# The first two rows of each partition stored from the scalar queue while the opening loads run: a top-2 expert dispatch

## The chip, the cores and the metric

The kernel runs on one core of one Trainium2 chip. The metric is the device time of one execution in microseconds (us); lower is better. A profile of one execution goes with it. Its span, from the first to the last instruction, is a little shorter than the device time, because the device time also holds the start and the end of the program.

Engines are named as the profile names them: DVE is VectorE, ACT is ScalarE, POOL is GpSimd, and SP is SyncE, which here only issues transfers. Each of the issuing engines has a queue of its own for DMA transfers; SPq stands for SP's issuing.

## The reference

For each of 16 x 1024 = 16,384 tokens, eight router logits give probabilities; the two largest are normalised to sum to one, and the token's row of 512 floats is written twice, scaled once by each of the two weights (the smaller first).

```python
def reference(x, router_logits, k):              # x: 16 x 1024 x 512, k = 2
    logits_max = np.max(router_logits, axis=-1, keepdims=True)
    probs = np.exp(router_logits - logits_max)
    probs = probs / np.sum(probs, axis=-1, keepdims=True)
    topk_indices = np.argsort(probs, axis=-1)[..., -k:]
    topk_probs = np.take_along_axis(probs, topk_indices, axis=-1)
    topk_probs = topk_probs / np.sum(topk_probs, axis=-1, keepdims=True)
    x_expanded = x[:, :, np.newaxis, :].repeat(k, axis=2)
    return (x_expanded * topk_probs[..., np.newaxis]).astype(np.float32)
```

Two of eight, normalised, need only the difference of the two largest logits and a sigmoid. What is left is movement: 33.6 MB of x are read, and 67.1 MB of output are written.

## The kernel before

Each of the 128 partitions holds 128 consecutive tokens ("rows"). A row of x is 2 KB, and a row of the output, with its two copies, is 4 KB. The rows are worked on in two groups of 64. A group's four loads of 16 rows fill the buffer `xs` (64 rows). Six multiplies make the output: 16 rows into the separate buffer `osp`, 16 rows into the lower half of `xs` itself (whose input has been used up by then), 8 and 8 rows into `osp` again, and 8 and 8 rows into the upper half of `xs`. Each is stored as soon as it is made. All transfers, loads and stores, are issued from the sync queue, in the order of the program.

```python
    GROUP = 64
    L = 16
    # ... x_v, o_v: partition p holds rows p*128 .. p*128+127
    logits = wpool.tile([P, M, E], F32)
    nc.sync.dma_start(logits, rl_v)
    WA = top2_weights(nc, wpool, logits, M, E)    # max/min tree on DVE, two sigmoids on ACT

    xs = wpool.tile([P, GROUP, D], F32)           # 64 rows, 128 KB in each partition
    osp = wpool.tile([P, L, 2, D], F32)           # 16 rows of output, 64 KB in each partition

    low = xs[:, : 2 * L, :].rearrange("p (r k) d -> p r k d", k=2)
    high = xs[:, 2 * L :, :].rearrange("p (r k) d -> p r k d", k=2)
    h = L // 2
    plan = [                                      # first row, rows, where the output is made
        (0, L, osp),
        (L, L, low),
        (2 * L, h, osp[:, :h]),
        (2 * L + h, h, osp[:, h:]),
        (3 * L, h, high[:, :h]),
        (3 * L + h, h, high[:, h:]),
    ]

    for g in range(M // GROUP):                   # two groups
        m0 = g * GROUP
        for r in range(0, GROUP, L):              # four loads of 16 rows
            nc.sync.dma_start(xs[:, r : r + L, :], x_v[:, m0 + r : m0 + r + L, :])
        for r, n, og in plan:
            rows = slice(m0 + r, m0 + r + n)
            nc.vector.tensor_tensor(
                og,
                xs[:, r : r + n, :].unsqueeze(2).to_broadcast([P, n, 2, D]),
                WA[:, rows, :].unsqueeze(3).to_broadcast([P, n, 2, D]),
                op=ALU.mult,
            )
            nc.sync.dma_start(o_v[:, rows], og)
```

The loads of the second group overwrite `xs`, so each of them waits for the stores that read that part of `xs`. The third multiply of a group overwrites the first half of `osp`, so it waits for the store of what the first multiply made.

Of the kernel before, what the change touches and what calls it, by code (L numbers as in the profile page):

```python
# [1 line left out]

# [4 lines left out]

F32 = mybir.dt.float32
ALU = mybir.AluOpType
ACTF = mybir.ActivationFunctionType  # L10
P = 128


def top2_weights(nc, pool, logits, M, E):

    hi, lo, n = None, None, E
    while n > 1:  # L20
        n //= 2
        if hi is None:
            a, b = logits[:, :, 0:n], logits[:, :, n : 2 * n]
            nhi = pool.tile([P, M, n], F32, tag=f"hi{n}")
            nlo = pool.tile([P, M, n], F32, tag=f"lo{n}")
            nc.vector.tensor_tensor(nhi, a, b, op=ALU.max)  # L26
            nc.vector.tensor_tensor(nlo, a, b, op=ALU.min)  # L27
        else:
            a, b = hi[:, :, 0:n], hi[:, :, n : 2 * n]
            nhi = pool.tile([P, M, n], F32, tag=f"hi{n}")  # L30
            nlo = pool.tile([P, M, n], F32, tag=f"lo{n}")
            tmp = pool.tile([P, M, n], F32, tag=f"tmp{n}")
            nc.vector.tensor_tensor(tmp, lo[:, :, 0:n], lo[:, :, n : 2 * n], op=ALU.max)  # L33
            nc.vector.tensor_tensor(nlo, a, b, op=ALU.min)  # L34
            nc.vector.tensor_tensor(nlo, nlo, tmp, op=ALU.max)  # L35
            nc.vector.tensor_tensor(nhi, a, b, op=ALU.max)  # L36
        hi, lo = nhi, nlo
    dlt = pool.tile([P, M], F32, tag="dlt")
    nc.vector.tensor_tensor(dlt, hi[:, :, 0], lo[:, :, 0], op=ALU.subtract)  # L39
    WA = pool.tile([P, M, 2], F32, tag="WA")  # L40
    nc.scalar.activation(WA[:, :, 0], dlt, ACTF.Sigmoid, scale=-1.0)  # L41
    nc.scalar.activation(WA[:, :, 1], dlt, ACTF.Sigmoid, scale=1.0)  # L42
    return WA


@with_exitstack
def kernel(
    ctx: ExitStack,
    tc: tile.TileContext,
    x: bass.AP,  # L50
    router_logits: bass.AP,
    k: bass.AP,
    out: bass.AP,
):
    nc = tc.nc
    B, S, D = x.shape
    E = router_logits.shape[-1]
    N = B * S
    assert int(k) == 2 and E == 8 and N % P == 0
    M = N // P  # L60

    GROUP = 64
    L = 16
    x_v = x.rearrange("b s d -> (b s) d").rearrange("(p m) d -> p m d", p=P)
    o_v = out.rearrange("b s k d -> (b s) k d").rearrange("(p m) k d -> p m k d", p=P)
    rl_v = router_logits.rearrange("b s e -> (b s) e").rearrange(
        "(p m) e -> p m e", p=P
    )

    wpool = ctx.enter_context(tc.tile_pool(name="wpool", bufs=1))  # L70
    logits = wpool.tile([P, M, E], F32)
    nc.sync.dma_start(logits, rl_v)  # L72
    WA = top2_weights(nc, wpool, logits, M, E)

    xs = wpool.tile([P, GROUP, D], F32)
    osp = wpool.tile([P, L, 2, D], F32)


    low = xs[:, : 2 * L, :].rearrange("p (r k) d -> p r k d", k=2)
    high = xs[:, 2 * L :, :].rearrange("p (r k) d -> p r k d", k=2)  # L80
    h = L // 2
    plan = [
        (0, L, osp),
        (L, L, low),
        (2 * L, h, osp[:, :h]),
        (2 * L + h, h, osp[:, h:]),
        (3 * L, h, high[:, :h]),
        (3 * L + h, h, high[:, h:]),
    ]

    for g in range(M // GROUP):
        m0 = g * GROUP
        for r in range(0, GROUP, L):
# [6 lines that stand above are left out]
                WA[:, rows, :].unsqueeze(3).to_broadcast([P, n, 2, D]),  # L100
                op=ALU.mult,
            )
            nc.sync.dma_start(o_v[:, rows], og)  # L103


# [1 line left out]
_INS = ['x', 'router_logits', 'k']  # L107
_OUTS = [((16, 1024, 2, 512), 'float32')]

_NUMBERS = {'k': 2}  # L110


# [26 lines left out]
```

## Time and profile before

| | |
|---|---|
| device time, median of 3 runs | 242.84 us (242.69 to 243.03) |
| device time of the profiled execution | 242.31 us |
| its span | 240.5 us |
| DVE busy | 142.0 us, 23 instructions |
| ACT busy | 1.8 us, 3 instructions |
| packets | 3,024, with 101.19 MB |
| multiply of 16 rows (16,384 elements in each partition) | 17.2 us |
| multiply of 8 rows (8,192 elements) | 8.7 us |
| load of 16 rows, 4,096 KB, issue to landing | 36.3 us, median of 8 |

In a profile, a line such as "DVE L97 TENSOR_TENSOR osp<-xs,WA" is an instruction of VectorE from line 97 that writes `osp` from `xs` and `WA`. The time from the issue of a transfer to its landing holds its wait behind the transfers ahead of it, so it is longer than the moving of its bytes alone. A row of digits gives the busy share, in tenths, of 40 equal slices of the span. The page's rate of data (GB/s) in a short slice can swing, as a packet's bytes are all counted where the packet starts.

### The profile page before, as it was taken

Reading aid. Unit: us, or ns where it says so; the run is one execution under the profiler, and the core shown is the slowest. Engines: PE = TensorE matmul, PEld = TensorE weight load, DVE = VectorE, ACT = ScalarE, POOL = GpSimd, SP = SyncE. Lnnn points to the kernel's source line nnn. Section 1 sums busy time; section 2 is a strip of 40 time slices with the busy share of each in tenths; the row PEclk is TensorE's granted clock in tenths of the full one; section 3 lists DMA queues with packets and bytes.
Section 4 is the critical chain, followed back from the end, with each engine's and each line's share of the span. In section 5 each row is a group of like instructions: output and inputs, shape, how many; then the busy total and the mean of one; then the engine's idle time right before and its main releaser. Section 6 shows DMA issues by size and latency. Waiting matters only on the chain.

```text
span 240.5 us, 112 instructions
## 1 busy us (share of the span) xinstructions
DVE 142.0 (59%) x23; ACT 1.8 (1%) x3; POOL 0.2 (0%) x4
## 2 busy tenths in 40 slices
DVE  3279999900399999400000899998007999990000
ACT  2000000000000000000000000000000000000000
POOL 0000000000000000000000000000000000000000
DMA  8999999898989899999999999999989898999995
GB/s 327 430 409 425 430 431 425 349 523 349 523 349 523 349 436 436 436 436 431 436 338 431 436 431 430 431 474 414 458 381 490 371 501 360 431 436 436 436 436 256
DMA packets 3024, 101.19 MB, mean 421 GB/s; under 512 B 336, under 2 KB 336, under 8 KB 464
## 3 DMA queue, kind: packets, MB, share of 16 engines
q1 hardware_dynamic: 3024, 101.19, 98.7%
HBM read 34.08 MB, written 67.11 MB: 421 GB/s over the span
## 4 chain that ended last, share of the span: by engine, by line
DMA 46%; DVE 36%; issue 7%; SPq 0%; DVEq 0%
DMA out_dram<-osp 27%; DVE osp L97 22%; DMA xs<-in_x_dram 19%; DVE xs L97 14%; SPq L72 0%; SPq L103 0%; DVEq L97 0%
## 5 line engine op out<-in xcount | busy, mean ns | idle before, releaser
L97 DVE TENSOR_TENSOR osp<-xs,WA 128x8192 f32<-128x8192 f32 (+1 forms) x6 | 69.0, 11534 | 70.1 <-DMA xs<-in_x_dram 40.3
L97 DVE TENSOR_TENSOR xs<-xs,WA 128x8192 f32<-128x8192 f32 (+1 forms) x6 | 69.2, 11536 | 0.2
L26 DVE TENSOR_TENSOR nhi<-logits 128x512 f32<-128x512 f32 x1 | 0.7, 693 | 4.0 <-DMA logits<-in_router_logits_dram 4.0
L41 ACT ACT_TABLE_LOAD x1 | 1.3, 1283 | 0.7 <-PEq L120 0.7
L36 DVE TENSOR_TENSOR nhi<-nhi 128x256 f32<-128x256 f32 (+1 forms) x2 | 0.7, 354 | 0.0
L34 DVE TENSOR_TENSOR nlo<-nhi 128x256 f32<-128x256 f32 (+1 forms) x2 | 0.7, 354 | 0.0
L33 DVE TENSOR_TENSOR tmp<-nlo 128x256 f32<-128x256 f32 (+1 forms) x2 | 0.7, 353 | 0.0
L35 DVE TENSOR_TENSOR nlo<-nlo,tmp 128x256 f32<-128x256 f32 (+1 forms) x2 | 0.7, 352 | 0.0
L27 DVE TENSOR_TENSOR nlo<-logits 128x512 f32<-128x512 f32 x1 | 0.7, 685 | 0.0
L41 ACT ACTIVATE WA<-dlt 128x128 f32<-128x128 f32 x1 | 0.3, 315 | 5.8 <-DVE dlt L39 5.8
L39 DVE TENSOR_TENSOR dlt<-nhi,nlo 128x128 f32<-128x128 f32 x1 | 0.3, 291 | 0.0
L42 ACT ACTIVATE WA<-dlt 128x128 f32<-128x128 f32 x1 | 0.3, 298 | 0.0
L120 POOL MEMSET const-bfloat16-1.0<- 128x1 bf16 x1 | 0.1, 101 | 0.0
L120 POOL MEMSET const-uint8-127<- 128x1 uint8 x1 | 0.1, 101 | 0.0
L120 POOL MEMSET const-float32-0.0<- 128x1 f32 x1 | 0.1, 98 | 0.2 <-issue 0.2
L120 POOL MEMSET const-float32-1.0<- 128x1 f32 x1 | 0.1, 98 | 0.0
## 6 DMA issues: line engine op xcount, KB each, us to landing
xs<-in_x_dram SPq DMA_DIRECT2D x8, 4096.0 KB, 36.3
out_dram<-osp SPq DMA_DIRECT2D x4, 4096.0 KB, 20.7
out_dram<-xs SPq DMA_DIRECT2D x4, 4096.0 KB, 22.7
logits<-in_router_logits_dram SPq DMA_DIRECT2D x1, 512.0 KB, 3.3
out_dram<-osp SPq DMA_DIRECT2D x2, 32.0
out_dram<-xs SPq DMA_DIRECT2D x2, 34.1
```

The source lines that it names most:

```text
L26: nc.vector.tensor_tensor(nhi, a, b, op=ALU.max)
L27: nc.vector.tensor_tensor(nlo, a, b, op=ALU.min)
L33: nc.vector.tensor_tensor(tmp, lo[:, :, 0:n], lo[:, :, n : 2 * n], op=ALU.max)
L34: nc.vector.tensor_tensor(nlo, a, b, op=ALU.min)
L35: nc.vector.tensor_tensor(nlo, nlo, tmp, op=ALU.max)
L36: nc.vector.tensor_tensor(nhi, a, b, op=ALU.max)
L39: nc.vector.tensor_tensor(dlt, hi[:, :, 0], lo[:, :, 0], op=ALU.subtract)
L41: nc.scalar.activation(WA[:, :, 0], dlt, ACTF.Sigmoid, scale=-1.0)
L42: nc.scalar.activation(WA[:, :, 1], dlt, ACTF.Sigmoid, scale=1.0)
L97: nc.vector.tensor_tensor(og, xs[:, r : r + n, :].unsqueeze(2).to_broadcast([P, n, 2, D]), WA[:, rows, :].unsqueeze(3).to_broadcast([P, n, ...
L120: nc = _bacc.Bacc("TRN2", target_bir_lowering=False, num_devices=1)
```

## The change

The first multiply of each group is cut in two: 2 rows, then the other 14. Each part gets a store of its own. In the first group the 2-row store is issued from the scalar queue instead of the sync queue. Its purpose is to let the first output leave for HBM while the opening loads are still running, without standing behind those loads in the sync queue. In the second group the 2-row store goes through the sync queue like the others (its first row is 64, not 0). Nothing else changes, and the computation stays whole.

```diff
     h = L // 2
+    e = 2
     plan = [
-        (0, L, osp),
+        (0, e, osp[:, :e]),
+        (e, L - e, osp[:, e:]),
         (L, L, low),
         (2 * L, h, osp[:, :h]),
         (2 * L + h, h, osp[:, h:]),
@@ in the loop over the plan @@
                 WA[:, rows, :].unsqueeze(3).to_broadcast([P, n, 2, D]),
                 op=ALU.mult,
             )
-            nc.sync.dma_start(o_v[:, rows], og)
+
+            queue = nc.scalar if rows.start == 0 else nc.sync
+            queue.dma_start(o_v[:, rows], og)
```

## The prediction

> **What bounds the kernel now.** I read the page's first three parts first, to see which engine is ever full.
>
> ```profile
> span 240.5 us, 112 instructions
> DVE 142.0 (59%) x23; ACT 1.8 (1%) x3; POOL 0.2 (0%) x4
> ...
> DMA  8999999898989899999999999999989898999995
> ...
> q1 hardware_dynamic: 3024, 101.19, 98.7%
> HBM read 34.08 MB, written 67.11 MB: 421 GB/s over the span
> ```
>
> VectorE (DVE) works 59% of the span. The 16 DMA engines are at 98.7%, on one queue (q1). The first digit of the DMA row is the start-up, the last the drain; nothing between shows a hole. Bytes are fixed by the problem, so the suspicion is that the kernel takes as long as 101.19 MB take.
>
> The chain of work that ended last seems to disagree (DVE 36%), so the waits come next: does a late VectorE ever leave the DMA engines without work? First the waits, then the timeline from 13 to 64 us (start, duration, engine, instruction):
>
> ```profile
> DVE osp L97 <- DMA xs<-in_x_dram: 40.3, 2, 34.3
> DVE osp L97 <- DMA out_dram<-osp: 29.8, 2, 15.7
> ...
> 13.79 17.23 DVE L97 TENSOR_TENSOR osp<-xs,WA 128x16384 f32<-128x16384 f32 x1 [5.98 <-DMA xs<-in_x_dram]
> 31.05 0.35 SPq L103 DMA_DIRECT2D out_dram<-osp  x1
> 31.05 17.22 DVE L97 TENSOR_TENSOR xs<-xs,WA 128x16384 f32<-128x16384 f32 x1
> 48.30 0.34 SPq L103 DMA_DIRECT2D out_dram<-xs  x1
> 63.95 8.69 DVE L97 TENSOR_TENSOR osp<-xs,WA 128x8192 f32<-128x8192 f32 x1 [15.67 <-DMA out_dram<-osp]
> ```
>
> VectorE waits for DMA, 40.3 + 29.8 us, never the reverse for long. The first store is issued at 31.05, but the four opening loads, issued by 3.0 us, are still draining: by the trace's packet records the last of them ends at 44.2 us, and the store's first packet starts at 43.4, right behind the loads on its engine. So the store was queued 12 us ahead of its turn. I checked the same for every later transfer (issue to landing is 20.2 to 42.9 us, while 4 MB need only 9.7): each is issued with at least one other still ahead of it. Counted from the packet records, the 16 engines together are idle 0.65 us on average between the first packet (1.75 us) and the last (239.2 us), nearly all of it in the uneven finish.
>
> Hence the sum: 2,048 packets of 32 KB at 1.213 us and 512 of 64 KB at 2.418 us, over 16 engines, are 155.3 + 77.4 = 232.6 us; the logits' 128 packets of 4 KB at 0.159 us add 1.3. That is 233.9 of the 237.4 us between first and last packet. The other 3.4 us are packets longer than usual: 0.4 us in the start-up, 1.48 us at 40 to 44 us (loads give way to stores), 1.31 us at 118 to 127 us (stores to loads), 0.15 us at 158 to 162 us (loads to stores again). The windows show the middle one (columns: stretch, us, busy time of DVE, ACT and POOL, clock, DMA share, GB/s):
>
> ```profile
> 44.20:63.50 19.30, 4.08 (x1) 0.00 (x0) 0.00 (x0) 1.00 1.00 435
> ...
> 117.50:128.00 10.50, 0.00 (x0) 0.00 (x0) 0.00 (x0) 1.00 1.01 381
> 128.00:156.20 28.20, 23.14 (x2) 0.00 (x0) 0.00 (x0) 1.00 0.99 429
> ```
>
> Stores alone move 435 GB/s, loads alone 429, and the stretch in which stores and loads of different engines meet 381.
>
> **What the Trainium skill says.** "DMA: Bandwidth & Descriptors", section "Issuing engines are not separate DMA queues": transfers started by the scalar, sync or gpsimd engine end on the same 16 DMA engines and interleave; a second issuer saves only sequencer time. The trace has little to save: SP's issues take 0.33 to 0.53 us each and overlap transfers. The same page, "Where 436 GB/s comes from", puts the fabric's ceiling at 435 GB/s; the 435 of the window above agrees, so the store stages have nothing left. The same page, "Queues, rings and completion order": an engine takes turns between its queue rows, a whole packet at a time. This kernel has one queue, so no run here shows it yet; my placing of the early store rests on it. "Perfetto Trace Analysis", section "DMA Optimizations", says that splitting may let the whole finish sooner if DMA engines are generally idle; here they are not.
>
> **The change part by part.**
>
> (1) VectorE, the split of 16 rows into 2 and 14, in both groups. 16,384 elements take 17.225 us and 8,192 take 8.690, so 1.0419 ns each plus 0.155 us. 2,048 elements: 2.29 us; 14,336: 15.09; together 17.38 instead of 17.23. The +0.15 us per group lies ahead of waits of 15.7 and 14.1 us for a store: hidden.
>
> (2) The early store, first group. VectorE ends the two rows at 13.79 + 2.29 = 16.1 us. ScalarE has been free since 8.4 us. SP's first issue at 0.73 had its first packet at 1.75, so packets start near 17.1. The store is 128 packets of 8 KB (2 rows x 2 copies x 2 KB), 8 for each engine. From the line through 4 KB (159 ns) and 32 KB (1,213 ns) one is 0.31 us. Alternating with load packets, 8 turns are 8 x (1.213 + 0.31) = 12.2 us: it lands near 29.5 us.
>
> (3) What that displaces. The loads lose 8 x 0.31 = 2.5 us: the second lands before 25 instead of 23.4, the third near 35.5 instead of 33.1, the fourth near 47 instead of 44.5. VectorE needs the second at 31.2 and the third at 64. The 14-row store, issued at 31.2, starts when the fourth load ends, 2.5 us later, and is shorter by 8 packets' 8 KB, 2.4 us. It lands where the whole store landed, 63.9 us, and from there on everything repeats. The early bytes are not extra transfer capacity; they have pushed others back.
>
> (4) Packet overhead. 64 KB at 2.418 becomes 8 KB at 0.310 plus 56 KB at 2.418 - 0.301 = 2.117: +9 ns, 8 times per engine, 0.07 us; with another completion record of 9 ns, 0.08 per group, 0.16 us in all. This lies on the bound.
>
> (5) The second group's 2-row store stays on the sync queue, behind loads; it gets only the overhead of (4).
>
> (6) The build's instruction order adds one condition to the third multiply: it waits for the early store as well as the 14-row store. By (2), 34 us before it matters. The rotation of DMA semaphores shifts by one per new transfer; every wait I followed is on a transfer that landed well earlier or was waited for anyway.
>
> Without mixing the sum is +0.16 us, 243.0.
>
> **Rivals.** *Reads and writes disturb each other.* In the stretch at 381 GB/s, against the 429 of the clean loads after it, 10.5 x (1 - 381/429) = 1.2 us are lost. The change makes some 12 us of interleaving from 17 to 29 us. At that rate it costs 12.2 x 0.112 = 1.4 us: 244.4. Worse: at 40 to 44 us each engine's last two load packets took about 2.0 us instead of 1.2. If all eight load packets between the early store's packets stretched by 0.75 us, that would be 6 us: 249. Against it: at 158 to 162 us some engines still loaded while others stored, for only 0.15 us. I put a few tenths into the central figure.
>
> *An easier turn from loads to stores.* If the 1.48 us at 40 to 44 us are the price of the first writes, starting them softly might save it: 241.5. Against it, the second turn cost a tenth of that with the same instructions, so the price is not fixed; and the turn is still there behind the early store.
>
> *The DMA engines read and write at once, so the early store rides free.* Then 8 x 0.31 = 2.5 us would be gained: 240.5. Against it: wherever engines work undisturbed, packets follow end to end, one at a time on each engine.
>
> *VectorE or a wait gets onto the path.* It would need over 10 us of delay to empty the queue; nothing here makes that.
>
> **Range and chances.** 243.0 plus some 0.2 us as the weighted share of mixing (loss likelier than gain) is 243.2. The times before span 0.34 us. The low end, 242.1, takes half of the cheaper turn; the high end, 245.2, the 1.4 us of mixing plus some. Faster by over 2% means below 238.0, hardly above the packets' floor of 233.9 plus both ends' 3.1 us: 0.02. Slower by over 2% means above 247.7, which only the harsh form of mixing reaches: 0.06. The rest, 0.92, is within.
>
> **What would show it.** A second DMA queue with 1.05 MB, its store issued near 16.1 and landing near 29.5 us (in step 2); were it near 19, it had priority, near 46, it stood behind the loads. Load packets stay at 1.213 us from 17 to 29 us (no mixing cost), or stretch. The third multiply starts at 63.9 +- 1.5 us, and DMA waits remain over 65 us. The stretch of 40 to 44 us, now near 46, says whether the turn got cheaper. I am wrong if the DMA row shows a hole, if load packets stretch over the whole interleaving, or if the span falls by over 2 us.

## The result and the profile after

The changed kernel takes 241.87 us (median of 4 runs, 241.72 to 241.93) where the kernel before took 242.94 us (median of 4, one run more than in the table of before; 242.69 to 243.37). The ratio is 0.9953, with a 95% interval of 0.9936 to 0.9970. The gain is small, and the interval is clear of 1. The forecast of 243.2 us had the wrong sign, and its low end of 242.1 us lies 0.23 us above the result. Measured again later, with 21 runs beside 43 of the kernel before, the ratio was 0.9983 (0.9976 to 0.9991), a gain of 0.4 us. These two intervals don't meet. The changed kernel's median hardly moved between the two comparisons (241.87 and 241.71 us), while the kernel before, at 242.94 us here, had medians of 242.16 to 242.35 us in all four later comparisons. So the 0.4 us are the better figure, and the first 1.07 us hold 0.6 to 0.8 us that belong to the first runs of the kernel before.

The page of the changed kernel, its first three parts:

```profile
span 240.2 us, 116 instructions
DVE 142.1 (59%) x25; ACT 1.8 (1%) x3; POOL 0.2 (0%) x4
...
DMA  7999999988989899999999999999999898999996
...
q1 hardware_dynamic: 3168, 100.14, 97.8%
q10 hardware_dynamic: 144, 1.05, 1.0%
HBM read 34.08 MB, written 67.11 MB: 421 GB/s over the span
```

The second queue (q10) is there with its 1.05 MB. The DMA row still has no hole, and the mean rate is the same 421 GB/s. Now the timeline of the changed kernel from 13 to 70 us, then the times from issue to landing of its first stores (in us, last column), then its longest waits:

```profile
13.92 17.29 DVE L99 TENSOR_TENSOR osp<-xs,WA 128x2048 f32<-128x2048 f32 x2 [6.05 <-DMA xs<-in_x_dram]
16.25 0.37 ACTq L107 DMA_DIRECT2D out_dram<-osp  x1
31.24 0.35 SPq L107 DMA_DIRECT2D out_dram<-osp  x1
...
63.21 8.69 DVE L99 TENSOR_TENSOR osp<-xs,WA 128x8192 f32<-128x8192 f32 x1 [14.74 <-DMA out_dram<-osp]
```

```profile
out_dram<-osp SPq DMA_DIRECT2D x2, 7168.0 KB, 31.8
out_dram<-osp ACTq DMA_DIRECT2D x1, 1024.0 KB, 16.6
```

```profile
DVE osp L99 <- DMA xs<-in_x_dram: 40.3, 2, 34.2
DVE osp L99 <- DMA out_dram<-osp: 29.3, 2, 14.7
```

The early store is issued at 16.25 us, as worked out, and lands at 16.25 + 16.6 = 32.9 us. The third multiply starts at 63.21 instead of 63.95 us. So 0.74 us have been won by then, where the forecast had nothing won. Other profiles agree: it starts at 63.95 to 64.05 us in three profiles of the kernel before, and at 63.17 us in a second one of the changed kernel. VectorE waits for DMA about as long as before, 69.6 us (70.1 before), which cost nothing then and cost nothing now.

**Where the time went.** One measure is used from here on. The packet records of a trace give each packet's duration, and a given size nearly always takes the same one: 4 KB 0.159 us, 8 KB 0.309, 16 KB 0.611, 32 KB 1.213, 56 KB 2.116, 64 KB 2.418. Whatever a packet takes beyond that, summed and divided by the 16 engines, is called *stretch*. It says how much later the engines are, on average, for packets that went slowly. As long as the engines have work throughout and end level, a stretch moves the end by as much. In the thirteen profiles of the table below this can be tried: the stretch after 14 us, taken from the mean end of the 16 engines, leaves 235.8 to 236.2 us each time.

The table gives the stretch in us by place; four more profiles are told in the text. The start-up before 14 us, with 0.26 to 0.62 us in each, is left out. "Early" is 14 to 32 us, where a small first store of the first group meets the loads; "turn 1" is 32 to 60 us, where the first group's loads end and its stores follow; "back" is where the second group's loads follow the first group's stores (75 to 133 us); "early 2" (133 to 150 us) and "turn 2" (150 to 170 us) are the same as "early" and "turn 1" in the second group. The last column is when the last of the 16 engines ended.

| kernel | early | turn 1 | back | early 2 | turn 2 | last end |
|---|---|---|---|---|---|---|
| before | 0.00 | 1.48 | 1.31 | 0.00 | 0.15 | 239.2 |
| before, again (two) | 0.01, 0.01 | 1.33, 1.37 | 0.66, 0.89 | 0.01, 0.00 | 0.48, 0.44 | 239.2, 239.2 |
| changed | 0.74 | 0.04 | 1.22 | 0.00 | 0.64 | 238.9 |
| changed, again | 0.64 | 0.00 | 1.20 | 0.00 | 0.18 | 238.5 |
| split, all on sync | 0.00 | 0.94 | 0.78 | 0.00 | 0.47 | 239.0 |
| first group only | 0.56 | 0.03 | 1.02 | 0.00 | 0.61 | 238.6 |
| both groups early | 0.57 | 0.00 | 0.77 | 0.37 | 0.01 | 238.2 |
| both groups early, again | 0.67 | 0.00 | 0.93 | 0.10 | 0.00 | 238.3 |
| both, 1 row | 0.16 | 0.66 | 0.97 | 0.00 | 0.24 | 238.5 |
| both, 4 rows | 1.07 | 0.00 | 0.87 | 0.72 | 0.00 | 239.8 |
| 8 rows, first group early | 1.03 | 0.89 | 0.73 | 0.00 | 0.33 | 240.0 |
| both early, one queue | 1.43 | 0.21 | 0.76 | 0.71 | 0.00 | 239.8 |

In the first group the kernel before pays 1.33 to 1.48 us in its three profiles, and the changed kernel 0.64 and 0.78. That is where the gain lies. The split's packet overhead takes 0.13 us back (the sum of all the usual durations is 234.10 us before and 234.23 after). The second group is as it was, apart from the wander of "back" and "turn 2", which differ by 0.3 to 0.65 us between profiles of one kernel. That is as much as the whole gain, so one profile alone would not show it; turn 1 wanders far less.

### The profile page after: what moved, and what is told of

Same layout as the page of the kernel before. It is cut to its first block, busy times and chain, and to the rows that moved or that the text cites. A ratio compares the mean times of both kernels' runs of the same rounds, so it can differ in the third digit from the quotient of the medians.

```text
span 240.2 us, 116 instructions
## 1 busy us (share of the span) xinstructions
DVE 142.1 (59%) x25; ACT 1.8 (1%) x3; POOL 0.2 (0%) x4
## 3 DMA queue, kind: packets, MB, share of 16 engines
q10 hardware_dynamic: 144, 1.05, 1.0%
## 4 chain that ended last, share of the span: by engine, by line
DMA 49%; DVE 32%; issue 7%; SPq 1%; DVEq 0%
DMA out_dram<-osp 26%; DMA xs<-in_x_dram 23%; DVE osp L99 18%; DVE xs L99 14%; SPq L96 0%; SPq L72 0%; SPq L107 0%; DVEq L99 0%
## 5 line engine op out<-in xcount | busy, mean ns | idle before, releaser
L99 DVE TENSOR_TENSOR osp<-xs,WA 128x8192 f32<-128x8192 f32 (+2 forms) x8 | 69.2, 8688 | 69.6 <-DMA xs<-in_x_dram 40.3
## 6 DMA issues: line engine op xcount, KB each, us to landing
out_dram<-osp ACTq DMA_DIRECT2D x1, 1024.0 KB, 16.6
```

What stands on the lines that cost most here:

```text
L99: nc.vector.tensor_tensor(og, xs[:, r : r + n, :].unsqueeze(2).to_broadcast([P, n, 2, D]), WA[:, rows, :].unsqueeze(3).to_broadcast([P, n, ...
```

## Experiments

Each changes the kernel before or the changed kernel by the lines shown, and the computation stays whole in all of them.

**Is it the split, the early store, or chance?** First, the split alone:

```diff
-            queue = nc.scalar if rows.start == 0 else nc.sync
+            queue = nc.sync
```

> Both splits into 2 and 14 rows kept, but every store from the sync queue, so that nothing is stored while the opening loads run. Theory (meeting the loads early is what helps: the first turn from loads to stores cost 1.48 us of stretched packets before, and 0.74 + 0.04 after): no gain left, ratio 1.000 to 1.001, and the stretch of about 1.5 us stands again at 40 to 44 us. Rival (the split helps: 8 KB packets at the head of the stores soften the turn): ratio 0.994 to 0.997 as with the whole change, and under 0.5 us of stretch at 40 to 44 us.

Measured: 242.19 us, ratio 1.0001 (0.9990 to 1.0012), and 0.94 us at turn 1. In time the split alone gives nothing, so the rival is out. The theory was not all right either: it had 1.5 us at turn 1. The 8 KB packets at the head of the stores may soften the turn (the third multiply starts at 63.67 us), and the overhead of 0.13 us takes part of that back; one profile can't settle it.

Next, the first group alone, with the second left unsplit:

```diff
-        for r, n, og in plan:
+        steps = plan if g == 0 else [(0, L, osp)] + plan[2:]
+        for r, n, og in steps:
```

> Only the first group is split, with its 2-row store from the scalar queue; the second group is as in the kernel before. Theory (early store alone): the whole gain, ratio 0.994 to 0.996, by 0.1 us better than the whole change because the second group's split overhead of 0.08 us is gone. Rival (the split): about half of the gain, 0.997 to 0.998.

And the whole change once more:

> The whole change again, beside the others on one chip. Both theories: ratio 0.994 to 0.997. A third theory, that the gain is the wander of the turns from run to run, expects a ratio that is not clear of 1.0, or packets stretched at other places than in the first profile (0.74 us at 18 to 24, 0.04 at 44, 1.21 at 118 to 126, 0.64 at 156 to 162 us).

Measured: 241.79 us, ratio 0.9984 (0.9975 to 0.9993), and 241.71 us, 0.9983 (0.9976 to 0.9991). Both numbers that I wrote down were too large, as they leaned on the first measurement. By the sizes they name, early_only even looks like the rival's half; but the comparison that counts is with the whole change measured beside it, and there the two are equal. So the whole gain is the early store of the first group. It is also clear of 1.0, and the stretch in the first group, 0.64 and 0.00 us, lies where it lay in the first profile, so it is no chance.

Then the second group's 2-row store from the scalar queue as well, measured twice:

```diff
-            queue = nc.scalar if rows.start == 0 else nc.sync
+            queue = nc.scalar if r == 0 else nc.sync
```

> The second group's 2-row store also goes from the scalar queue, so it too meets its group's loads (issued near 134 us, loads until 162 us). Theory (early meeting makes a turn cheap): a second gain where the second turn is dear; with 0.15 to 0.64 us at that turn, at most 0.6 us less, but the early meeting costs up to 0.7 us of its own: ratio 0.992 to 0.997. If only the very first write of the kernel is dear, nothing more is gained: the ratio of the whole change plus 0 to 0.003. The rival (the split) expects the same as the whole change.

> Both groups' 2-row stores from the scalar queue, again, beside its variants. If the early meeting is worth something at each turn: ratio 0.9955 to 0.998, better than the whole change by about 0.001, and no stretch of over 0.15 us near 44 and 160 us. If the first result was the wander of the runs: 0.9976 to 0.9991, as the whole change had on that chip.

Measured: 241.23 us, 0.9967 (0.9955 to 0.9979), and 241.30 us, 0.9966 (0.9954 to 0.9978). The same treatment pays again at the second turn, which falls to 0.01 and 0.00 us, for 0.37 and 0.10 us at the new early meeting: 0.38 and 0.10 us in all, where the turn alone cost 0.15 to 0.64 us in the versions without it. So it is not only the very first write that is dear. This version beats both kernels: beside its 241.23 us, the changed kernel took 241.71 us in the same comparison. Its page, second profile, and its early stores:

```profile
span 239.5 us, 116 instructions
...
q1 hardware_dynamic: 3024, 99.09, 96.7%
q10 hardware_dynamic: 288, 2.10, 2.1%
HBM read 34.08 MB, written 67.11 MB: 423 GB/s over the span
...
out_dram<-osp ACTq DMA_DIRECT2D x2, 1024.0 KB, 16.6
```

**Is the dear turn the rule?** The kernel before, twice more, for its turns:

> The kernel before once more, for its turns alone. If the first turn from loads to stores is dear as a rule: 0.9 to 1.5 us near 40 to 44 us. If 1.48 us was chance: under 0.8 us. The turn near 159 us, 0.15 us before, shows how far a turn wanders.

> The same again: 0.9 to 1.5 us near 40 to 44 us, or under 0.8 us if the first was chance.

1.33 and 1.37 us at the first turn: it is the rule. The second turn, 0.48 and 0.44 us, shows that the 0.15 of the first profile, on which the forecast leaned, was at the low end of what this turn costs: where the second group's first store is not early, it lies anywhere from 0.15 to 0.64 us in the table.

**Does more of it help?** I thought that a second queue's alternation would make every turn cheap, whatever the size. First the unsplit 16-row store from the scalar queue:

```diff
-            nc.sync.dma_start(o_v[:, rows], og)
+            queue = nc.scalar if rows.start == 0 else nc.sync
+            queue.dma_start(o_v[:, rows], og)
```

> No split; the first group's whole 16-row store (64 KB packets) goes from the scalar queue. It is issued near 31 us, while some 9 of the 128 load packets of each engine... counted from 31 to 44 us, are still to come, so it alternates with them. Theory (a turn is cheap where the two directions alternate from two queues, whatever the size): ratio 0.997 to 0.999, and no stretch of over 0.3 us where the loads end. Rival (it needs small packets, or a start long before the loads end): ratio 0.9995 to 1.001, with 0.9 to 1.5 us of stretched packets in all between 30 and 60 us.

(Each engine has 32 load packets in a group, not 128.) Measured: 243.50 us, ratio 1.0050 (1.0033 to 1.0068). The theory falls in this form. Stretch is 1.34 us at turn 1, at 32 to 37 us, where the store meets the loads: as dear as before. After that, 32 KB loads and 64 KB stores alternate at their usual durations. And one engine ends at 241.0 us, 1.9 us after the next.

The other extreme, all stores from the scalar queue (`queue = nc.scalar`):

> No split; all twelve stores from the scalar queue, all loads from the sync queue, so that stores and loads alternate at every change of direction, also where the second group's loads follow the first group's stores (1.0 to 1.3 us of stretch near 119 to 126 us so far). Theory: all three turns get cheap, total stretch 1.2 to 2.2 us instead of 2.6 to 3.4, ratio 0.993 to 0.998. Rival (each change costs much the same wherever it lies): stretch of 2.5 us or more in other places, ratio 0.999 to 1.003.

Measured: 245.06 us, ratio 1.0100 (1.0077 to 1.0123). Neither theory had this ratio. The total stretch, 3.55 us, is the rival's "2.5 us or more", but not the whole loss. The windows near the end show the rest (stretch, us, busy DVE, ACT, POOL, clock, DMA share, GB/s):

```profile
231.00:237.00 6.00, 0.00 (x0) 0.00 (x0) 0.00 (x0) 1.00 1.01 437
237.00:243.40 6.40, 0.00 (x0) 0.00 (x0) 0.00 (x0) 1.00 0.29 123
```

In the last 6.4 us the engines are busy for 29% only: nine have ended by 237.8 us, the others between 239.9 and 243.3. After a long alternation the engines are no longer level, and the slowest sets the end. In the kernel before all 16 end within 1.1 us. This profile and the one before it are of the slowest executions of their kernels (246.43 and 244.20 us), so the usual unevenness may be smaller. Why single engines fall behind I did not trace.

A second queue that meets no loads at first, the store from the lower half of the buffer (`queue = nc.scalar if rows.start == L else nc.sync`):

> No split; only the second store of the first group (from the lower half of the load buffer, issued near 48 us, when the loads have ended) goes from the scalar queue. Theory (what helps is meeting the loads): no gain, ratio 0.9995 to 1.001, with 0.9 to 1.5 us of stretch at 40 to 44 us. Rival (a second queue helps by itself, by more work at hand for the engines): ratio 0.997 to 0.999.

Measured: 246.23 us, ratio 1.0166 (1.0150 to 1.0181), the largest loss of all, and neither theory had it. The waits, two lines of the timeline and a window of this run:

```profile
DVE osp L97 <- DMA out_dram<-osp: 54.7, 3, 26.9
```

```profile
75.75 17.29 DVE L97 TENSOR_TENSOR osp<-xs,WA 128x8192 f32<-128x8192 f32 x2 [26.95 <-DMA out_dram<-osp]
...
84.47 8.95 SPq L104 DMA_DIRECT2D out_dram<-osp  x2
```

```profile
82.00:84.20 2.20, 2.20 (x1) 0.00 (x0) 0.00 (x0) 1.00 0.46 134
```

The two big stores alternate, so the one that VectorE waits for lands late: its third multiply starts at 75.75 instead of 63.95 us, behind a wait of 26.9 us. What it makes is stored from 84.47 us on, and the queues run dry meanwhile: from 82.0 to 84.2 us the DMA engines are busy for 46%. Where loads and stores start anew, at 82 to 94 us, 1.93 us of stretch lie on load packets, against 0.66 to 1.31 us at "back" in the kernel before. What the forecast had ruled out for the change, VectorE getting onto the path, happens here, through nothing but the order of two stores.

**How much should be stored early?** 8 rows instead of 2 (`e = 8` in the changed kernel):

> The first store has 8 rows instead of 2 (in both groups; from the scalar queue in the first): it is issued near 22.7 us, has packets of 32 KB, and alternates with the loads until about 47 us. Theory (the price of the early meeting is a transient of 0.6 to 0.7 us once, and alternation then costs nothing): the same ratio as with 2 rows, 0.997 to 0.999, with stretch only in the first 5 us or so after the issue. Rival (every alternated packet costs): three or four times the early cost, 2 us or more, and ratio 1.003 to 1.006.

Measured: 243.16 us, ratio 1.0040 (1.0026 to 1.0053). Between the two theories: the price is a transient (1.03 us at 24 to 27 us, then usual durations), not one for each packet; but turn 1 keeps 0.89 us, and the last engine ends at 240.0 us. Then 1 and 4 rows, early in both groups (`e = 1` and `e = 4`):

> As that, with 1 row (4 KB packets) instead of 2. So far the price of the first meeting with the loads was 0.56 to 0.74 us with 8 KB packets, 1.02 with 32 KB and 1.22 and 1.28 us with 64 KB. Theory (it grows with the size of the packets that meet the loads): 0.3 to 0.55 us here, ratio 0.995 to 0.998. Rival (it is the same for any size, and those were chance): 0.6 to 1.2 us. A second rival (too little is stored early to make the later turn cheap): 0.5 us or more of stretch near 44 us, ratio 0.998 to 1.001.

> As that, with 4 rows (16 KB packets). Theory (size of the packets): 0.7 to 1.0 us at the first meeting, ratio 0.997 to 1.000. Rival (the same for any size): not to be told from 2 rows.

Measured: 241.71 us, 0.9980 (0.9972 to 0.9988) with 1 row; 242.65 us, 1.0019 (1.0012 to 1.0025) with 4. The early price in the first group goes 0.16, 0.57 to 0.67, 1.07 and 1.03 us with 1, 2, 4 and 8 rows, so it grows with the packet up to 16 KB. One row is too little, as the second rival had it: turn 1 keeps 0.66 us. Early and turn together are 0.82, 0.57 to 0.67, 1.07 and 1.92 us: two rows are the best of these. (Amount and packet size grow together here; these runs do not part them.) With 4 rows the stretch in the first group, 1.07 us, is still under the 1.33 to 1.48 of before, yet the kernel is slower: the second early meeting costs 0.72 us, and here, too, the last engine ends 0.5 us behind the next.

**Two queues, or only early?** The 2-row store early, but from the sync queue, between the second and the third load:

```diff
-        for r in range(0, GROUP, L):
-            nc.sync.dma_start(xs[:, r : r + L, :], x_v[:, m0 + r : m0 + r + L, :])
-        for r, n, og in plan:
-            ...   # multiply, store
+        load(0)
+        load(L)
+        step(*plan[0])          # 2 rows: multiply, store, all stores from the sync queue
+        load(2 * L)
+        load(3 * L)
+        for p in plan[1:]:
+            step(*p)
```

(`load` and `step` hold the lines taken out; their definitions are left out here.)

> Both groups' 2-row stores are early, but from the sync queue: each is issued after the group's second load and before its third, so that the 8 KB packets stand as one block between two loads, and nothing alternates. Theory (an early store makes the later turn cheap, whichever queue): under 0.15 us near 46 us, 0.5 to 1.0 us at the early store itself, ratio 0.996 to 0.998 as with the scalar queue. Rival (it is the alternation of two queues): the early block costs two turns of its own, and the later turn keeps 0.5 us or more: ratio 1.000 to 1.004.

Measured: 242.84 us, ratio 1.0024 (1.0012 to 1.0035). Its timeline:

```profile
16.48 0.35 SPq L106 DMA_DIRECT2D out_dram<-osp  x1
16.87 0.91 SPq L96 DMA_DIRECT2D xs<-in_x_dram  x2
31.48 0.34 SPq L106 DMA_DIRECT2D out_dram<-osp  x1
```

The store is issued as early as in the changed kernel, and the third load in good time behind it. The later turns become cheap here as well, 0.21 and 0.00 us: that follows from an early store, whichever the queue. But the early block costs 1.43 us, which is the full price of a turn, where the alternating store cost 0.56 to 0.74. In the packet records, each engine's last two load packets ahead of the block take 2.05 and 1.8 us on average; ahead of the alternating packets of the changed kernel they take about 1.4 and 1.55. Each theory is half right: being early makes the later turn cheap, and the second queue makes being early cheap. Of these versions only those with both gain.

**The other direction.** A 2-row load of the second group from the scalar queue, while the first group's stores run, on top of the version with both groups early:

```diff
         for r in range(0, GROUP, L):
-            nc.sync.dma_start(xs[:, r : r + L, :], x_v[:, m0 + r : m0 + r + L, :])
+            lo_r = r
+            if g > 0 and r == 0:
+                nc.scalar.dma_start(xs[:, :e, :], x_v[:, m0 : m0 + e, :])
+                lo_r = e
+            nc.sync.dma_start(xs[:, lo_r : r + L, :], x_v[:, m0 + lo_r : m0 + r + L, :])
```

> As with 2 rows, and the first 2 rows of the second group's first load (packets of 4 KB) come from the scalar queue too, near 82 us, while stores run, 37 us ahead of the turn from stores to loads that has cost 0.8 to 1.3 us near 119 to 126 us. Theory (an early meeting makes the later turn cheap in this direction too): under 0.4 us at that turn, and up to 0.7 us near 82 us; ratio 0.993 to 0.997. Rival (only the turn to stores can be made cheap): the turn keeps 0.8 us or more, and the early load adds its own price; ratio 0.997 to 1.000.

Measured: 241.36 us, ratio 0.9967 (0.9954 to 0.9979), the same as without it. The turn from stores to loads keeps its 0.97 us, at 122 to 129 us, and the early load has no visible price. So its theory falls: that turn is not bought off in this way. Its second 2-row store went out at 100.3 us, among stores, and turn 2 was 0.28 us instead of 0.00, which fits: that store did not meet the loads.

## Why the prediction was wrong

**What bounds the kernel** held. The DMA row shows no hole, VectorE's waits are about as long as before and cost nothing, and the floor of 233.9 us for the packets has moved by no more than the overhead of (4).

**(1), the split multiplies**, held: 17.29 us for the pair, and hidden.

**(2), the early store**, held for the issue (16.25 against 16.1 us) and the alternation: packet records show one 8 KB packet, then one load packet, in turns, as the Trainium skill's "DMA: Bandwidth & Descriptors", section "Queues, rings and completion order", has it, but for one place near 24 us, where two 8 KB packets follow each other. The step that failed in size was the start: not near 17.1 but near 20.9 us, because two more load packets passed first on each engine, and slowly. From the first early packet to the end of the last it then took 10.4 us, less than the 12.2 of the forecast, as only six load packets, not eight, ran between an engine's eight early ones. The landing came 1.6 us after the end of the last packet (31.3 us), which the forecast had left out. Together it landed at 32.9 and not 29.5 us.

**(3), what it displaces**, is where the forecast broke. "It lands where the whole store landed, 63.9 us" was 63.2 us. The bytes did push others back, as claimed, but the last load packet ended at 45.8 us, 1.6 us later than before and not 2.5: the sum kept the turn's 1.48 us in place, and it measured 0.04, at a price of 0.74 us for the early meeting. The rival named "an easier turn from loads to stores" at 241.5 us was the right one, and I turned it down with two reasons. One, that the second turn cost a tenth, so that the price wasn't fixed, rested on a single profile: in two others that turn cost three times as much, and the first turn was 1.33 and 1.37 us again. The other, that "the turn is still there behind the early store", was wrong: it costs 0.00 to 0.04 us there.

**The cost of mixing** was sized by the wrong rule. I took 11.2% of the time for as long as loads and stores alternate, 1.4 us. The measured price is one transient of 0.56 to 0.74 us in the first 6 us or so, and nothing after. A window in the middle of the alternation and one of loads alone, both of the changed kernel:

```profile
24.50:30.50 6.00, 6.00 (x1) 0.00 (x0) 0.00 (x0) 1.00 1.02 440
128.00:156.00 28.00, 23.77 (x3) 0.00 (x0) 0.00 (x0) 1.00 1.00 432
```

The alternation moves no less than loads alone. The low rate of 381 GB/s in the stretch from 117.5 to 128 us, from which I took the 11.2%, was a turn, not a mixture. It is still there in the changed kernel:

```profile
117.50:128.00 10.50, 0.00 (x0) 0.00 (x0) 0.00 (x0) 1.00 1.03 396
```

**(4), packet overhead**, was 0.16 us in the forecast and is 0.13 us by the packet records. **(5) and (6)** held: the second group's 2-row store through the sync queue changed nothing that can be seen, and no new wait ended last.

The sum by the traces: -0.7 us in the first group (1.33 to 1.48 becomes 0.64 to 0.78), +0.13 us overhead, so some -0.55 us; the large repetition measured -0.4 us. The first measurement's -1.07 us is more than the traces explain. The profiled execution of the kernel before took 242.31 us there, below all four of its timed runs (242.69 and up), so the trace before doesn't hold the part that made those slower. What that part was stays open. Set against the later comparison, the low end of the forecast, 0.74 us under the kernel before, would have held the gain of 0.4 us; the central figure would still have had the wrong sign. The statement of the Trainium skill's "DMA: Bandwidth & Descriptors", section "Issuing engines are not separate DMA queues", that a second issuer saves only sequencer time, is too narrow for this case by measurement: which queue a store came from moved this kernel by between -0.3% and +1.7%.

Also open is the mechanism itself: why the load packets ahead of the first stores go slowly, why an early store takes that away from a turn over 10 us later, and why 8 rows early did not. The runs show the prices; none shows what happens inside.

## What to carry to other kernels

In a kernel whose DMA engines are always busy, look for packets that take longer than others of their size: here 3.4 us of 240 lay there, 2.9 of them where the direction of transfer changes. In this kernel a small store from a second queue, early enough to alternate with the loads, roughly halved the price of the first turn (best with 8 KB packets; both groups so treated gave a ratio of 0.9966), while big ones gave it back, and an alternation between two stores can delay just the one that someone waits for (1.0166). Before sizing an effect from one place in one profile, see a second profile of the same kernel: the turn that I leaned on cost 0.15 us in one and 0.44 and 0.48 us in two others.

## What the runs showed that I had not expected

A change of direction on all 16 DMA engines costs 1.33 to 1.48 us at this kernel's first turn, and the slow packets are the last two loads of each engine, ahead of the stores' first packets. Alternation of single packets, of 8 KB beside 32 KB and of 64 KB beside 32 KB, runs at the usual durations once it has begun. And loads and stores that alternate for long from two queues can leave the 16 engines uneven: they ended within 1.1 us of each other before, within 3.4 us with one 16-row store from the second queue, and within 6.0 us with all stores there.
